# The first block of a recurrence issued in one step, and filling products issued ahead of the normed outputs' steps

## The chip, the cores and the metric

One Trainium2 chip, one core. The time is the device time of one execution in microseconds (us), as a median over runs. A profiled execution gives, beside its own time, the span from its first to its last instruction and every instruction's start and duration. The engines are TensorE (PE; its weight loads are listed as PEld), VectorE (DVE), ScalarE (ACT), GpSimd (POOL) and the queue that issues DMAs (SP).

## The reference

One layer of a residual block on 512 frames of width 1024, in float32: a SwiGLU feed-forward half step, a mixer, and a second SwiGLU half step. Each reads an RMS-normed, scaled and shifted copy of `x` and adds its gated output to `x`. The mixer has two groups of four heads each:

- attention heads (low-rank q and kv, rotary part, block-causal), whose outputs are RMS-normed;
- gated delta-rule heads. A state `S` of 128 x 128 per head goes through the sequence chunk by chunk:

```python
def step(state, inp):
    u_c, wk_c, qd_c, kd_c, qk_c, gl_c = inp
    v_new = u_c - wk_c @ state
    o_c = qd_c @ state + qk_c @ v_new
    state = state * gl_c + kd_c.T @ v_new
    return state, o_c        # the state starts at zero
```

Their outputs are RMS-normed per head and multiplied by SiLU of a gate. `mixed @ w_out`, with both groups side by side, is the mixer's output.

## The kernel before, in words

Activations lie feature-major, 512 frames wide, in 128-row tiles. Each large product is made of three matmuls (`mm3`, L466 to L470): both operands are split into a high and a low part, and high-high, high-low and low-high are accumulated in PSUM. The splits of weights are a ScalarE copy and a VectorE subtraction (L228, L229).

The recurrence uses blocks of 128 frames, so there are four, p = 0 to 3, each with four heads side by side in 512 columns. What happens around it:

- `bases`, `inverse`, `inverse_levels` invert the triangular matrices (L1905 is the last batch of their matmuls). `solve(p)` makes `us[p]` (L1931, copied at L1933) and, from block 1 on, `wk[p]` (L1940, L1942).
- `recur(p)` is a generator of two parts. The first reads the state: `wk` times `S` (L1966), `vn` (L1968), `S` scaled on GpSimd, `q` times `S` (L1974) and its copies on ScalarE (L1976). The second makes the new state (L1981, `S` at L1984 for block 0, L1986 for others) and the block's output (L1989, added at L1993, or copied at L1991 for block 0). Block 0 has no state: its first part issues nothing, but yields.
- `gated_out(p)` norms the output in three steps: squares, sums and the reciprocal root on GpSimd (L2027, L2028, L2003, L214); the scaling `on` (L1475); then transposes (L2012), the gate (`mf`, L2018) and the split into `mh` and `ml` (L2020, L2021), eight pieces on VectorE in all.
- `attended(h)` finishes an attention head in the same way (transposes L2211, `mh` L2216, `ml` L2217).
- `out_attended` are the filling products, called `fill`: w_out's rows for the attention heads, 8 output tiles x 4 heads = 32 steps. A step is one group of three matmuls of 512 columns; every fourth is followed by the update of `x` (L2386). When they are done, `out_half` follows (256 columns, the delta-rule heads, first two blocks), then `out_rest`.
- `early` splits the first weights of the second feed-forward (`fh`, `fl`, L1470, L1471): three generators of three steps, of which the third does nothing; their loads are issued when they are listed.

These are stepped by the loop at the end of `mixer`. `Side.step` advances a list of generators. `gate()` issues the gates' SiLU once attention is done, and afterwards steps the normed outputs (`gated`). What order results:

- TensorE executes in the order in which its instructions are planned. Inside `matmuls_in_order` each matmul is tied behind the one traced before it, except those that `loosely` traces (the remaining solves and attention heads).
- On the other engines, and for loose matmuls, the planner takes at each point the instruction that was traced first among those that its own estimate of times holds ready. Tiles of PSUM (`psb`, 5 banks; `psa`, 3) and SBUF slots are given out in the same pass. So a changed trace order can change the order on VectorE and ScalarE too.

Before the loop one early step is taken; in block 0's first pass the last attention head is finished and `fill` begins.

Of the kernel before, what the change touches and what calls it, by code (L numbers as in the profile page):

```python
# [96 lines left out]
class Block:  # L97
# [1855 lines left out]
    def recur(self, p):  # L1953

        nc = self.nc
        h4 = lambda x: x.rearrange("p (h d) -> p h d", h=4)
        hs = lambda h: slice(h * P, (h + 1) * P)
        S, last = self.S, p == NB - 1
        ts = slice(p * P, (p + 1) * P)
        o = self.slot(s="o")  # L1960
        if S is None:
            vn = self.us[p]
        else:
            pw = self.aux()
            for h in range(4):
                nc.tensor.matmul(pw[:, hs(h)], self.wk[p][:, hs(h)], S[:, hs(h)], start=True, stop=True)  # L1966
            vn = self.slot(s="vn")
            nc.vector.tensor_tensor(out=vn, in0=self.us[p], in1=pw, op=ALU.subtract)  # L1968
            if not last:
                sg = self.slot(s="Sg")  # L1970
                self.mul(h4(sg), h4(S), self.bc(self.gl[:, 4 * p:4 * p + 4], 4), nc.gpsimd)
            pq = self.aux()
            for h in range(4):
                nc.tensor.matmul(pq[:, hs(h)], self.qT[h][:, ts], S[:, hs(h)], start=True, stop=True)  # L1974
            for h in range(4):
                nc.scalar.activation(o[:, hs(h)], pq[:, hs(h)], AF.Copy, scale=self.eG[:, 4 * p + h:4 * p + h + 1])  # L1976
        yield
        if not last:
            pst = self.aux()
            for h in range(4):  # L1980
                nc.tensor.matmul(pst[:, hs(h)], self.kd[p][:, hs(h)], vn[:, hs(h)], start=True, stop=True)  # L1981
            self.S = self.slot(s="S")
            if S is None:
                nc.vector.tensor_copy(self.S, pst)  # L1984
            else:
                nc.vector.tensor_tensor(out=self.S, in0=sg, in1=pst, op=ALU.add)  # L1986
        po = self.aux()
        for h in range(4):
            nc.tensor.matmul(po[:, hs(h)], self.qk[h][:, ts], vn[:, hs(h)], start=True, stop=True)  # L1989
        if S is None:  # L1990
            nc.scalar.copy(o, po)  # L1991
        else:
            nc.vector.tensor_tensor(out=o, in0=o, in1=po, op=ALU.add)  # L1993
        self.o[p] = o
        yield
# [224 lines left out]
    def mixer(self, norms):  # L2220
# [81 lines left out]
        fill = Side()  # L2302
# [9 lines left out]
        def gate_silu(n):  # L2312
            silu(gates[:n], self.att_end)
            del gates[:n]
# [15 lines left out]
        def loosely(side, n):  # L2330
            with self.traced() as block:
                side.step(n)
            self.loose.update(i.name for i in block)

        self.mixed[:4] = [(self.slot(F32R, "mh"), self.slot(F32R, "ml")) for _ in range(4)]
        with self.matmuls_in_order():
            gated, self.gated = Side(), 0

            def gate(n=1):
                if gates and not (att.open or att.todo):  # L2340
                    gate_silu(4)
                elif not gates:
                    gated.step(n)

            for p in range(NB):
                while self.wk[p] is None:
                    loosely(chain, 1)
                for _ in self.recur(p):
                    loosely(chain, 2)
                    loosely(rest, 4)  # L2350
                    gate()
                    early.step()
                    if not rest.open and not rest.todo:
                        fill.step(3)
                gated.add(self.gated_out(p))
                gate()
                if p == 1:
                    def half():
                        while self.gated < 2:
                            yield  # L2360
                        yield from self.out_half()
                    fill.add(half())
            while rest.open or rest.todo:
                loosely(rest, 1)
            gate_silu(4)
            early.flush()
            fill.step(2)
            gated.step()
            fill.step(4)
            gated.flush()  # L2370
            fill.flush()
        with self.in_order({mybir.EngineType.PE: self.last_mm}):
# [99 lines left out]
```

## Time and profile before

| | |
|---|---|
| median of 3 runs | 1030.54 us (1029.92 to 1031.6) |
| profiled execution: time, span | 1030.97 us, 1029.3 us |
| TensorE busy | 1013.7 us (98%) |
| VectorE busy | 774.0 us (75%) |
| ScalarE busy | 504.7 us (49%) |
| GpSimd busy | 30.0 us (3%) |
| recurrence, L1981 of block 0 to L2012 of block 3 | 609.4 to 646.8 us |
| granted TensorE clock | 1.000 |

A row of the order in time reads: start, duration, engine, line, operation, output <- inputs, shape, count, and in brackets how long the engine stood idle before it and what it waited for. Matmuls overlap: the start of one lies before the modelled end of the one ahead, so distances between starts say more than durations. A wait is listed as "engine tile line <- what it waited for: sum, times, longest".

### The profile page before, as it was taken

How to read it: one execution, taken by the hardware profiler on the slowest of the kernel's cores; microseconds unless marked ns; L12 is line 12 of the kernel's file. 1: busy time of each engine (PE TensorE's matmuls, PEld its weight loads, DVE VectorE, ACT ScalarE, POOL GpSimd, SP SyncE). 2: the span in 40 equal slices, each digit the busy share in tenths (PEclk: the TensorE clock that was granted, in tenths of full speed). 3: DMA queues.
4: the chain of work that ended last, by engine and by line, in shares of the span. 5: the costliest groups of instructions: out<-in, count | busy, mean ns of one | idle time of the engine just before them, and what ended most of it. 6: DMA issues, size and time to landing. Idle time of an engine off the chain costs nothing. (4 is left out here: it accounts for less than half of the span.)

```text
span 1029.3 us, 16966 instructions
## 1 busy us (share of the span) xinstructions
PE 1013.7 (98%) x6663; PEld 906.4 (88%) x6663; DVE 774.0 (75%) x1355; ACT 504.7 (49%) x911; POOL 30.0 (3%) x74
## 2 busy tenths in 40 slices
PE   7999999999999999999999989999999999999998
PEld 6788899999887899888888788998999999987887
DVE  4789788887787847868888558677888888788541
ACT  4452455556322226469854464374555555633330
POOL 0000000001100000000000011000000000000000
PEclk9999999999999999999999999999999999999999
DMA  9987234244688735211321121113333334383421
GB/s 321 296 277 255 72 93 122 84 124 117 203 296 297 254 92 160 74 42 42 75 75 42 42 83 41 42 40 95 92 100 106 108 99 120 110 277 93 128 61 31
DMA packets 203773, 130.77 MB, mean 127 GB/s; under 512 B 14241, under 2 KB 188334, under 8 KB 203694
## 3 DMA queue, kind: packets, MB, share of 16 engines
q1 hardware_dynamic: 203694, 129.70, 41.5%
q8 instruction: 52, 0.85, 0.3%
q14 instruction: 27, 0.22, 0.1%
HBM read 127.18 MB, written 2.49 MB: 126 GB/s over the span
## 5 line engine op out<-in xcount | busy, mean ns | idle before, releaser
L228 ACT CAST wh<-wr 128x1024 fp32r<-128x1024 f32 (+1 forms) x93 | 93.8, 1016 | 143.3 <-PE pa L469 108.6
L269 DVE TENSOR_TENSOR wl<-wr,wh 128x1024 fp32r<-128x1024 f32 x96 | 117.4, 1223 | 54.5 <-ACT wh L273 54.5
L229 DVE TENSOR_TENSOR wl<-wr,wh 128x1024 fp32r<-128x1024 f32 (+1 forms) x93 | 108.9, 1177 | 45.5 <-ACT wh L228 45.0
L468 PE MATMUL pa<-hh,wh 128*128 128x512 f32 (+1 forms) x357 | 137.4, 385 | 0.0
L470 PE MATMUL pa<-hh,wl 128*128 128x512 f32 (+1 forms) x357 | 135.2, 379 | 0.0
L469 PE MATMUL pa<-hl,wh 128*128 128x512 f32 (+1 forms) x357 | 134.6, 377 | 0.0
L468 PE MATMUL pa<-ah,wh 128*128 128x512 f32 (+1 forms) x356 | 132.3, 372 | 0.0
L469 PE MATMUL pa<-al,wh 128*128 128x512 f32 (+1 forms) x356 | 131.1, 368 | 0.0
L470 PE MATMUL pa<-ah,wl 128*128 128x512 f32 (+1 forms) x356 | 130.9, 368 | 0.0
L273 ACT CAST wh<-wr 128x1024 fp32r<-128x1024 f32 x96 | 98.2, 1054 | 18.3 <-PE pa L469 10.4
L837 DVE SCALAR_TENSOR_TENSOR aa<-ar,sc,aa 128x512 f32<-128x512 f32 x98 | 73.4, 749 | 8.3 <-DMA ar<-in_w_ada 6.5
L468 PEld LDWEIGHTS pa<-hh,wh 128*128 128x128 f32 x357 | 67.4, 189 | 13.1 <-issue 2.5
L468 PEld LDWEIGHTS pa<-ah,wh 128*128 128x128 f32 x356 | 67.1, 188 | 13.5 <-ACT wh L228 2.5
L470 PEld LDWEIGHTS pa<-hh,wl 128*128 128x128 f32 x357 | 67.2, 188 | 11.9
L470 PEld LDWEIGHTS pa<-ah,wl 128*128 128x128 f32 x356 | 67.1, 188 | 11.2
L469 PEld LDWEIGHTS pa<-hl,wh 128*128 128x128 f32 x357 | 67.4, 189 | 10.7
L469 PEld LDWEIGHTS pa<-al,wh 128*128 128x128 f32 x356 | 67.1, 189 | 10.7
L354 PE MATMUL pa<-hh,wh 128*128 128x256 f32 x240 | 68.0, 283 | 0.0
L354 PE MATMUL pa<-th,wh 128*128 128x256 f32 x240 | 67.9, 283 | 0.0
L354 PE MATMUL pa<-tl,wh 128*128 128x256 f32 x240 | 67.9, 283 | 0.0
L354 PE MATMUL pa<-th,wl 128*128 128x256 f32 x240 | 67.9, 283 | 0.0
L354 PE MATMUL pa<-hh,wl 128*128 128x256 f32 x240 | 67.9, 283 | 0.0
(480 smaller groups left out, 2487.1 us busy)
## 6 DMA issues: line engine op xcount, KB each, us to landing
wr<-in_ffn_w_in SPq DMA_DIRECT2D x79, 512.0 KB
ar<-in_w_ada SPq DMA_DIRECT2D x96, 256.0 KB
wr<-in_ffn_w_out SPq DMA_DIRECT2D x32, 512.0 KB
ar<-in_w_ada SPq DMA_DIRECT2D x22, 512.0 KB
wr<-in_w_in SPq DMA_DIRECT2D x21, 512.0 KB
wr<-in_ffn_w_out SPq DMA_DIRECT2D x16, 384.0 KB
wr<-in_w_out SPq DMA_DIRECT2D x8, 512.0 KB
wr<-in_ffn_w_in SPq DMA_DIRECT2D x8, 384.0 KB
```

The source lines that it names most:

```text
L228: self.nc.scalar.copy(hi, raw)
L229: self.nc.vector.tensor_tensor(out=lo, in0=raw, in1=hi.bitcast(F32), op=ALU.subtract)
L269: sub = lambda out, x, y: nc.vector.tensor_tensor(out=out, in0=x, in1=y, op=ALU.subtract)
L273: nc.scalar.copy(hi[:, :n], raw[:, :n])
L354: nc.tensor.matmul(z, a[:, j, :], b, start=start and j == 0 and i == 0, stop=j == 3 and i == 2, skip_group_check=not start)
L468: mm(out, wh, xh, start=start, stop=False)
L469: mm(out, wh, xl, start=False, stop=False)
L470: mm(out, wl, xh, start=False, stop=stop)
L837: nc.vector.scalar_tensor_tensor(out=acc, in0=a, scalar=sc, in1=acc, op0=ALU.mult, op1=ALU.add)
```

## The change

Three things are changed.

1. `recur` yields after its first part only where there is a state. Block 0 is issued in one step, so the loop's body runs 7 times and not 8.
2. In the body, `gate()` comes behind the filling products and not ahead of them, and `early` isn't stepped in block 0.
3. Behind the loop, six filling steps and not four stand between the last block's scaling and its transposes.

```diff
@@ recur @@
             for h in range(4):
                 nc.scalar.activation(o[:, hs(h)], pq[:, hs(h)], AF.Copy, scale=self.eG[:, 4 * p + h:4 * p + h + 1])
-        yield
+            yield
         if not last:
             pst = self.aux()
@@ mixer @@
                 for _ in self.recur(p):
                     loosely(chain, 2)
                     loosely(rest, 4)
-                    gate()
-                    early.step()
+                    if p:
+                        early.step()
                     if not rest.open and not rest.todo:
                         fill.step(3)
+                    gate()
                 gated.add(self.gated_out(p))
                 gate()
                 if p == 1:
@@ mixer @@
             early.flush()
             fill.step(2)
             gated.step()
-            fill.step(4)
+            fill.step(6)
             gated.flush()
             fill.flush()
```

## The prediction

> **What bounds the kernel now.** I read the page's first two lines, then the stretches around the recurrence, then what TensorE waited for, then the order of instructions on each engine there. The page's lines:
>
> ```profile
> span 1029.3 us, 16966 instructions
> ...
> PE 1013.7 (98%) x6663; PEld 906.4 (88%) x6663; DVE 774.0 (75%) x1355; ACT 504.7 (49%) x911; POOL 30.0 (3%) x74
> ```
>
> TensorE is busy 1013.7 of 1029.3 us, so a change that neither adds nor removes a matmul can win at most its idle time, 15.6 us. The stretches (start:end, length, busy time of PE, PEld, DVE, ACT, POOL, granted clock, DMA) say where that lies:
>
> ```profile
> 593.90:599.40 5.50, 5.10 (x51) 4.25 (x50) 3.26 (x8) 3.29 (x9) 1.01 (x1) 1.00 1.07 326
> 599.40:617.50 18.10, 15.40 (x121) 14.34 (x122) 9.12 (x16) 11.87 (x22) 2.05 (x2) 1.00 0.05 14
> 617.50:637.00 19.50, 19.50 (x128) 17.45 (x126) 16.36 (x38) 10.46 (x28) 4.91 (x4) 1.00 0.10 28
> 637.00:650.00 13.00, 10.71 (x59) 8.99 (x59) 11.46 (x28) 4.39 (x11) 1.01 (x2) 1.00 0.28 82
> 650.00:675.00 25.00, 24.91 (x209) 24.71 (x208) 16.84 (x41) 9.45 (x22) 0.70 (x1) 1.00 0.07 22
> ```
>
> Two stretches have holes, 2.70 and 2.29 us. Between them and after them TensorE has none to speak of (19.50 of 19.50, 24.91 of 25.00), so time won at the holes should reach the end. The clock is full in all of them. TensorE's waits from 585 to 650 us, longest first:
>
> ```profile
> PE pb L2012 <- DVE on L1475: 2.3, 2, 1.5
> PE pb L1966 <- DVE S L1984: 1.5, 1, 1.5
> PE pb L2211 <- DVE on L1475: 1.2, 1, 1.2
> PE pb L2189 <- DVE U L1909: 0.4, 1, 0.4
> ```
>
> L2012 transposes a block's normed output, L1966 is the first product of a recurrence block, L2211 the last attention head's transposes. Where they stand, with the end of the matmul order of before:
>
> ```profile
> 593.95 0.48 PE L468 MATMUL pa<-mh,wh 128*128 128x512 f32 x1
> ...
> 594.73 0.40 PE L468 MATMUL pa<-mh,wh 128*128 128x512 f32 x1
> ...
> 595.51 2.08 PE L1905 MATMUL pb<-U,Y 64*64 64x64 f32 x32
> ...
> 606.79 0.48 PE L468 MATMUL pa<-mh,wh 128*128 128x512 f32 x1
> ...
> 608.91 0.63 PE L2211 MATMUL pb<-ident,on 128*128 128x128 f32 x4 [1.19 <-DVE on L1475]
> 609.38 1.06 PE L1981 MATMUL pb<-uu,kd 128*128 128x128 f32 x8
> 610.27 1.06 PE L1989 MATMUL pb<-uu,qk 128*128 128x128 f32 x8
> ...
> 615.76 1.13 PE L1966 MATMUL pb<-S,w 128*128 128x128 f32 x8 [1.47 <-DVE S L1984]
> ...
> 636.00 1.05 PE L1989 MATMUL pb<-vn,qk 128*128 128x128 f32 x8
> 637.88 0.63 PE L2012 MATMUL pb<-ident,on 128*128 128x128 f32 x4 [0.82 <-DVE on L1475]
> 638.26 0.47 PE L468 MATMUL pa<-mh,wh 128*128 128x512 f32 x1
> ...
> 644.28 0.39 PE L470 MATMUL pa<-mh,wl 128*128 128x512 f32 x1
> 646.14 0.66 PE L2012 MATMUL pb<-ident,on 128*128 128x128 f32 x4 [1.47 <-DVE on L1475]
> ```
>
> The holes are 1.19 + 1.47 + 0.82 + 1.47 = **4.95 us**. The filling products come in groups of three matmuls (L468 to L470); nine of them stand between the last two L2012, from 638.26 to 644.28 + 0.23, so one group is 0.69 us. There are 32 groups before the half-width ones.
>
> **The change part by part.**
>
> *One step for block 0.* Block 0 has no state to read, so the first part of its generator issues nothing; before, the loop still ran its body there, with three groups. They are the ones at 593.95, 594.73 and 606.79. As the loop's matmuls keep their traced order, L1981 of block 0 had to stand behind the third. Now L1981 and L1989 are first in that order and the three groups follow them. Two prices:
>
> The loss. The two groups at 593.95 can no longer be there, since L1981 needs `uu`, which ScalarE copies eight microseconds later. They covered a wait:
>
> ```profile
> 594.56 0.59 ACT L1898 COPY Y<-pb 64x512 f32<-64x512 f32 x1
> ...
> 602.61 0.59 ACT L1933 COPY uu<-pb 128x512 f32<-128x512 f32 x1 [1.06 <-PE pb L1931]
> ...
> 595.51 1.94 PEld L1905 LDWEIGHTS pb<-U,Y 64*64 64x64 f32 x32 [0.36 <-ACT Y L1898]
> ```
>
> L1905 starts when ScalarE's copy is in, groups or not, so the place stays 595.51 and 2 x 0.69 = **1.38 us** of products must be done later. Nothing else stands ready behind them: all later matmuls of the loop are ordered behind L1989. The bounds: at best other loose products (attention's transposes) slip in and nothing is lost, 0; at worst 1.56, the whole 593.95 to 595.51. I take 1.38, the groups' own length.
>
> The gain. L1981 and L1989 (609.38 to 611.16, 1.78 us) move in front of the solves of blocks 2 and 3, and the three groups (2.07 us) stand free to run while L2211 waits for `on`, 1.19 us. For L1966 the profile shows what kept `S`, on VectorE:
>
> ```profile
> 612.95 0.75 DVE L2386 SCALAR_TENSOR_TENSOR xT<-pa,mod,xT 128x512 f32<-128x512 f32 x1 [1.89 <-PE pa L470]
> 614.32 0.69 DVE L1471 TENSOR_TENSOR fl<-fr,fh 128x512 fp32r<-128x512 f32 x1 [0.62 <-ACT fh L1470]
> 614.93 0.68 DVE L1984 COPY S<-pb 128x512 f32<-128x512 f32 x1
> ```
>
> `S` was ready to copy at about 610.4 and was queued behind the first residual update, which waited 1.89 us for the fourth group, and behind a split of an early weight, which waited for ScalarE. Now that fourth group comes behind L1966 and L1974 of block 1, so its update can't stand ahead of `S`, and the split (early.step) isn't taken in block 0 at all. Both holes close: **1.19 + 1.47 = 2.66**. Bounds: 0, if L2211 and `S` are planned as late as before, to 2.66. I take 2.66: behind L1989 there are 2.07 us of groups, eight matmuls of L1940 (0.89, as L1981's eight from 609.38 to 610.27) and L2211's four (0.47) in front of L1966, against 0.68 for the copy. The split left out costs the same 0.69 us later, in the flush behind the loop, under the eight groups there; without them it would stand in the last block's chain. The gates' SiLU moves behind the groups; on ScalarE it waits for the last head anyway. No DMA passes another: the early weights' loads are all issued when their list is made, the groups issue their weights' loads in the same order on SP, and the steps that they pass issue none.
>
> *Groups in front of the normed outputs' steps.* In each pass the three groups now come ahead of gate(), so a block's L2012 stands three groups (2.07 us) later behind L1989. Blocks 0 and 1 waited for nothing. Block 2 waited **0.82** at 637.88 and has 2.07 more: gone.
>
> *Six groups at the last.* Between L1989 of block 3 and its L2012 there stood 9 groups, one L2012 and the 0.82 wait; now 3 + 2 + 6 = 11 groups and one L2012, 11 x 0.69 + 0.38 = 7.97 us. On VectorE the last block's chain ran so:
>
> ```profile
> 638.90 0.68 DVE L1993 TENSOR_TENSOR o<-o,pb 128x512 f32<-128x512 f32 x1
> ...
> 642.32 0.68 DVE L2028 TENSOR_REDUCE gs<-hn 128x4 f32<-128x512 f32 x1
> 642.91 1.22 DVE L229 TENSOR_TENSOR wl<-wr,wh 128x1024 fp32r<-128x1024 f32 x1
> ...
> 645.39 0.69 DVE L1475 TENSOR_TENSOR on<-o,ry 128x512 f32<-128x512 f32 x1 [0.52 <-POOL ry L214]
> ```
>
> From L1989's end (637.05) to `on` (646.08) are 9.03 us, of which 1.85 pass before `o` starts (block 2's late `on` stands ahead) and 2.74 between `o` and `gs`, where ScalarE's square takes 0.63 and block 2's eight pieces and an update the rest:
>
> ```profile
> 639.70 0.63 ACT L2027 ACTIVATE hn<-o 128x512 f32<-128x512 f32 x1 [3.90 <-DVE o L1993]
> ```
>
> With block 2's `on` long done and its transposes 2.07 us behind L1989, `o` can start at once, and `gs` is ready 1.6 us behind L1989 (0.68 + 0.63 and the hops), before those pieces exist. Without these two delays the chain needs 9.03 - 1.85 - (2.74 - 0.75) = about 5.2 us against 7.97: the wait of **1.47** goes. Bounds: +1.47 to a loss of 0.83 (second rival). I take 1.47, since the order of readiness is what the planner goes by.
>
> *The sum:* 4.95 - 1.38 = 3.57 us. The profiled execution took 1030.97 with a span of 1029.3; it becomes 1025.7 in span and 1027.4 in time. It stands 0.43 above the median of the runs, 1030.54, so for the median I say **1027.0 us**. No matmul is added; 3.57 us of waiting go.
>
> **The rivals.**
>
> *The last transposes still wait.* If VectorE's order stays as it was, with block 3's squares behind block 2's pieces, the 8.20 us from L2012 at 637.88 to `on` at 646.08 stay, and the cover behind that L2012 is only 0.38 + 8 x 0.69 = 5.9: a wait of 2.3 in place of 1.47. Then 4.95 - 1.38 - 2.3 = 1.27, or 1029.3 us. For it: pieces come earlier in the program than the squares. Against it: they are ready about a microsecond later.
>
> GpSimd's rsqrt is in this chain:
>
> ```profile
> 634.91 1.22 DVE L229 TENSOR_TENSOR wl<-wr,wh 128x1024 fp32r<-128x1024 f32 x1
> ...
> 635.14 1.86 POOL L214 TENSOR_TENSOR ry<-ve,mhalf 128x4 f32<-128x4 f32 x1 [6.47 <-DVE ve L2003]
> ...
> 644.35 1.01 POOL L214 TENSOR_TENSOR ry<-ve,mhalf 128x4 f32<-128x4 f32 x1 [7.35 <-DVE ve L2003]
> ```
>
> It took 1.86 instead of 1.01 us while a weight split ran on VectorE. If that meets the last one too, 0.85 more comes on: 1030.1 in this rival, nothing in the forecast, which has 2.8 us to spare. [...]
>
> *The first half does nothing.* If L2211 and `S` are planned late for a reason other than the one I read, both holes stay and only the second stretch is won: 0.82 + 1.47 - 1.38 = 0.91, or 1029.6 us. The move to the front of the order speaks against it.
>
> *VectorE becomes the bound: slower.* L2012 now stands right ahead of the next block's L1966, so block p's pieces meet `vn` of block p+2. Their rows:
>
> ```profile
> L2018 DVE SCALAR_TENSOR_TENSOR mf<-pb,cwT,z 128x128 f32<-128x128 f32 x16 | 4.9, 346 | 0.8 <-PE pb L2012 0.8
> L2021 DVE TENSOR_TENSOR ml<-mf,mh 128x128 fp32r<-128x128 f32 x16 | 4.1, 287 | 0.2 <-ACT mh L2020 0.2
> ```
>
> Four of each are 4 x (0.35 + 0.29) = 2.5 us. From L2012's end TensorE has L1966, L1974 and three groups, 1.78 + 2.07 = 3.85 us, before L1981 needs `vn`. Pieces and `vn` (0.69) fit, 3.2; with a weight split (1.22) and an update (0.75) ahead, 5.2, they don't, and 1.35 is waited for in blocks 2 and 3 each, 2.7. With the last transposes late too (a full VectorE makes both) it is 4.95 - 1.38 - 2.3 - 2.7 = -1.43: 1032.0 us. It decides from 0.65 us a block on. For it: VectorE is busy 16.36 of 19.50 in that stretch. Against it: 3.14 are free, and the work is the same, only later by three groups.
>
> **How the numbers follow.** Forecast 0.55 (1026.4 to 1027.9, by what the loss at 593.95 and small delays on VectorE make of it), last transposes 0.20, first half nothing 0.15, slower 0.10. The best end is the loss at 0 and everything closed, 4.95: 1025.6. The upper end takes in the second and third case: 1030.2. About 0.2% (2.1 us) is what a measurement of this kernel tells from no change. The forecast lies below 1028.5, as does a small part of the second case, where some of the wait is left: faster 0.60. The rest of the second, the third, and a third of the slower one (shorter stalls) are within: 0.33. Slower 0.07.
>
> **What would show it.** Right: no group of filling products before L1981 of block 0; a hole of about 1.5 us before L1905; no wait at L2211 and at the first L1966; none at the last two L2012; from 650 on the same steps some 3.6 us earlier. Wrong: a new wait of L1981 for `vn`, of the last L2012 for `on`, or anything in the hole before L1905 that I say can't be there; and a shift that is given back later would be against my reading that TensorE is full behind 650.

## The result, and the profile after

The changed kernel takes **1028.65 us** (median of 16 runs, 1026.54 to 1030.84), the kernel before 1030.59 beside it (16 runs, 1029.92 to 1032.26): a ratio of 0.998, 95% interval 0.9973 to 0.9987. It is faster, by 1.9 us and not by the forecast's 3.5, and by a little less than the 2.1 us that the prediction takes for what a measurement here tells from no change. The profiled execution took 1027.16 us with a span of 1025.4; it is one of the shorter ones.

The first two lines of its page:

```profile
span 1025.4 us, 16972 instructions
...
PE 1014.4 (99%) x6663; PEld 907.5 (88%) x6663; DVE 774.0 (75%) x1355; ACT 504.4 (49%) x911; POOL 29.8 (3%) x74
```

The stretches of the prediction (length, busy time of PE, PEld, DVE, ACT, POOL, granted clock, DMA), and the single microseconds inside the first:

```profile
593.90:599.40 5.50, 4.89 (x44) 4.65 (x45) 3.49 (x9) 2.31 (x5) 1.01 (x1) 0.71 1.07 325
599.40:617.50 18.10, 18.01 (x141) 17.05 (x141) 9.13 (x16) 13.45 (x26) 3.06 (x3) 0.99 0.01 3
617.50:637.00 19.50, 19.50 (x124) 17.01 (x123) 17.80 (x40) 9.63 (x24) 3.44 (x3) 1.00 0.12 35
637.00:650.00 13.00, 13.00 (x84) 11.62 (x83) 11.69 (x30) 5.69 (x14) 1.32 (x1) 1.00 0.28 83
...
595.00:596.00 1.00, 1.00 (x21) 1.00 (x19) 0.82 (x2) 0.49 (x2) 0.00 (x0) 1.00 1.08 317
596.00:597.00 1.00, 1.00 (x12) 0.88 (x10) 0.03 (x1) 0.00 (x0) 0.89 (x1) 0.60 1.10 327
597.00:598.00 1.00, 1.00 (x6) 1.00 (x7) 0.84 (x2) 0.00 (x1) 0.12 (x1) 0.50 1.14 343
598.00:599.00 1.00, 1.00 (x6) 1.00 (x5) 1.00 (x4) 0.63 (x2) 0.00 (x0) 0.50 1.14 344
599.00:600.00 1.00, 1.00 (x8) 0.88 (x7) 1.00 (x3) 0.63 (x3) 0.00 (x0) 0.69 0.36 107
```

The two stretches with holes are full now (18.01 of 18.10, 13.00 of 13.00). But the granted clock, 1.00 in every stretch of before, is 0.71 in the first: it stands at 0.50 from about 596.2 to 599.6. What TensorE waited for from 580 to 655 us is one row:

```profile
PE pb L1905 <- ACT Y L1898: 1.0, 1, 1.0
```

All four of the old waits are gone, and L2189's 0.4 as well. The order of TensorE in the stretches of the change, after:

```profile
593.08 0.44 PE L2183 MATMUL pb<-ident,pr 128*128 128x128 f32 x2
594.51 2.30 PE L1905 MATMUL pb<-U,Y 64*64 64x64 f32 x32 [0.99 <-ACT Y L1898]
596.74 1.22 PE L2189 MATMUL pb<-vn,pT 128*128 128x128 f32 x4
597.75 1.70 PE L2183 MATMUL pb<-ident,pr 128*128 128x128 f32 x7
599.25 2.04 PE L2189 MATMUL pb<-vn,pT 128*128 128x128 f32 x14
601.12 0.60 PE L2211 MATMUL pb<-ident,on 128*128 128x128 f32 x4
...
608.96 0.63 PE L2211 MATMUL pb<-ident,on 128*128 128x128 f32 x4
...
611.51 1.05 PE L1966 MATMUL pb<-S,w 128*128 128x128 f32 x8
...
632.68 1.16 PE L1989 MATMUL pb<-vn,qk 128*128 128x128 f32 x8
...
641.68 0.64 PE L2012 MATMUL pb<-ident,on 128*128 128x128 f32 x4
```

and before, at the same instructions:

```profile
593.75 0.44 PE L2183 MATMUL pb<-ident,pr 128*128 128x128 f32 x2
...
597.52 0.71 PE L2189 MATMUL pb<-vn,pT 128*128 128x128 f32 x4
598.07 0.93 PE L2183 MATMUL pb<-ident,pr 128*128 128x128 f32 x7
599.44 1.80 PE L2189 MATMUL pb<-vn,pT 128*128 128x128 f32 x14 [0.44 <-DVE U L1909]
601.08 0.60 PE L2211 MATMUL pb<-ident,on 128*128 128x128 f32 x4
```

The same instructions last up to 1.8 times as long: four L2189 1.22 for 0.71, seven L2183 1.70 for 0.93. From the start of L1905 to the start of L2211 it is 594.51 to 601.12, 6.61 us, where before took 595.51 to 601.08, 5.57: **1.04 us lost**, with the closed wait of 0.44 in it already.

The whole time of one execution hides much of this. The two transposes ahead of L1905 (the L2183 x2 above), which stand ahead of everything that the change moves, start anywhere between 592.81 and 595.19 us in the 13 profiles of this study. So I also measure from their start to an instruction behind the mixer, VectorE's scaling of the next norm's sums:

```profile
661.95 0.16 DVE L805 TENSOR_SCALAR ve<-pb 128x2 f32<-128x2 f32 x1 [1.74 <-PE pb L754]
```

in before, and in the changed kernel:

```profile
658.16 0.16 DVE L805 TENSOR_SCALAR ve<-pb 128x2 f32<-128x2 f32 x1 [1.74 <-PE pb L754]
```

From there to the end all 13 profiles take 367.2 to 367.4 us. Between the two points before takes 68.20 us and the changed kernel 65.08: **3.12 us won** in this execution, against 3.57 forecast. L805 comes 3.79 us earlier, and the end 3.81: nothing is given back later.

### The profile page after: what moved, and what is told of

Read it like the earlier page. It is cut to its first block, busy times and chain, and to the rows that moved or that the text cites. A ratio compares the mean times of both kernels' runs of the same rounds, so it can differ in the third digit from the quotient of the medians.

```text
span 1025.4 us, 16972 instructions
## 1 busy us (share of the span) xinstructions
PE 1014.4 (99%) x6663; PEld 907.5 (88%) x6663; DVE 774.0 (75%) x1355; ACT 504.4 (49%) x911; POOL 29.8 (3%) x74
## 4 chain that ended last, share of the span: by engine, by line
PE 92%; DVE 4%; ACT 1%; SPq 1%; DMA 1%; issue 0%; POOL 0%; ACTq 0%; DVEq 0%
PE pa L354 17%; PE pa L468 17%; PE pa L469 16%; PE pa L470 16%; PE pb L354 13%; PE pa L1250 1%; PE pb L2189 1%; PE pb L1250 1%; PE pb L468 1%; PE pb L469 1%; PE pb L470 1%; SPq L136 1%; DMA ar<-in_w_ada 1%; PE pb L2169 1%; DVE cv L1687 1%; DVE wl L229 1%
## 5 line engine op out<-in xcount | busy, mean ns | idle before, releaser
L354 PE MATMUL pa<-hl,wh 128*128 128x256 f32 x240 | 67.9, 283 | 0.0
```

The source lines that it names most:

```text
L354: nc.tensor.matmul(z, a[:, j, :], b, start=start and j == 0 and i == 0, stop=j == 3 and i == 2, skip_group_check=not start)
```

## The experiments

Two theories stood after the result. *Clock:* the loss is the half clock behind the new hole before L1905, and the hole sets it off; fill the hole with anything and the forecast's time appears. *Order:* the loss comes from VectorE and the DMAs in the new order, and the low clock only goes along with it. Each run is timed against the kernel before on the same chip.

**The changed kernel once more**, with no edit.

> The changed kernel once more, for its spread. Theory A (the clock): the hole of about 1.4 us that the change opens before L1905 lets the granted TensorE clock fall to one half for some microseconds in most executions, and that costs the median some 1.6 us and makes the times spread; so times from 1026.5 to 1031, median about 1028.6, and the lowest times go with a mean clock of 1.000. Theory B (the order): the missing gain and the spread come from VectorE and the DMAs in the new order, and the lower clock goes along with it; the same median, but no tie between clock and time.

1027.89 us (11 runs), ratio 0.9974 (0.9965 to 0.9983), 0.7 below what either theory expected. Its profile has a clock of 0.996 for the whole, and its windows:

```profile
594.00:595.00 1.00, 0.67 (x9) 0.67 (x10) 0.15 (x2) 0.95 (x3) 0.00 (x0) 0.85 1.10 337
...
595.00:600.00 5.00, 5.00 (x37) 4.84 (x35) 3.83 (x9) 1.05 (x3) 1.01 (x1) 0.50 0.92 271
...
600.00:601.00 1.00, 1.00 (x6) 0.92 (x5) 0.28 (x1) 0.63 (x3) 0.00 (x0) 0.50 0.01 3
601.00:602.00 1.00, 1.00 (x9) 1.00 (x9) 0.46 (x1) 0.77 (x2) 0.00 (x0) 0.74 0.00 0
```

and in its order of matmuls:

```profile
594.33 3.39 PE L1905 MATMUL pb<-U,Y 64*64 64x64 f32 x32 [1.00 <-ACT Y L1898]
...
602.42 0.60 PE L2211 MATMUL pb<-ident,on 128*128 128x128 f32 x4
```

The same hole, but twice the half clock: 0.3 + 5 + 1 + 0.52 = 6.8 us of it (each window's missing clock divided by 0.5), where the first profile has 0.8 + 1 + 1 + 0.62 = 3.4. From L1905 to L2211 it is 8.09 us, 2.52 more than before. From L2211 to L805 the two profiles agree: 57.04 and 57.05 us. So the 1.5 us between them lie where the half clock stands, not in an order behind it.

Over the 27 executions of the changed kernel: five kept a clock of 1.000 and took 1027.40 us in the mean, eight show 0.998 (1027.89), fourteen 0.997 or 0.996 (1028.98). The tie is loose in so few runs: of the three of this run at 1.000, one is the fastest and two stand at its median. All 48 runs of the kernel before that were timed beside the experiments show 0.999 or more.

**The two groups loose again**, so that they may stand in the hole:

```diff
                     if not rest.open and not rest.todo:
-                        fill.step(3)
+                        if not p:
+                            loosely(fill, 2)
+                        fill.step(3 if p else 1)
                     gate()
```

> As the changed kernel, but the first two groups of filling products aren't tied behind L1989 of block 0, so they stand before L1905 again, as in the kernel before. Theory A: clock 1.000 in every execution, all of the 4.95 us won, 1025.6 us, and a spread as small as that of the kernel before (about 2 us). Theory B: the groups' 1.38 us are won and nothing else, about 1027.3 us, with the spread of the changed kernel.

1026.42 us (5 runs), ratio 0.996 (0.9948 to 0.9973), clock 0.999 or more in all five; timed once more, 1026.73. TensorE's only wait left is the L2189 of before. It is the fastest kernel of the study, but the time lies between what the two theories expected, 1025.6 and 1027.3, and the edit moves work too, so it doesn't tell them apart alone.

**One group loose** (`loosely(fill, 1)`, then two).

> As the changed kernel, but one group of the two stands before L1905, so the hole is half as long, about 0.7 us. Theory A: if half the hole keeps the clock up, 1030.6 - 4.95 + 0.69 = 1026.3 us with a clock of 1.000; if it doesn't, 1027.9 with a clock below 1.000. Theory B: 0.69 below the changed kernel, 1027.9, with the same spread.

1026.70 us (6 runs), 0.9965 (0.9953 to 0.9977), clock 0.999 or more. The wait at L1905 is 0.3 and another of 0.8 stands at L2189, 4 us later: about the same idle time as the changed kernel's, in two pieces, and no half clock.

**The hole filled with work that is thrown away.** Everything stays as in the changed kernel; two extra groups, whose sums the next product overwrites, may run in the hole (the products that count are unchanged):

```diff
             p = self.acc()
+            if t == 0:
+                for _ in range(2):
+                    self.dense(p, u[0], self.mixed[4:], k1=1, last=0)
+                yield
             for k in range(4):
@@ mixer @@
                     if not rest.open and not rest.todo:
+                        if not p:
+                            loosely(fill, 1)
                         fill.step(3)
```

> As the changed kernel, with two groups of matmuls whose results are thrown away in the hole before L1905: they compute the first group twice into a tile that the true first group starts anew. No other instruction changes its place. Theory A: the clock stays at 1.000, and the time is that of the forecast, 1030.6 - 3.57 = 1027.0 us, 1.6 below the changed kernel, with a small spread, though more work is done. Theory B: useless work wins nothing, 1028.6 us with the same spread.

1027.14 us (8 runs), 0.997 (0.996 to 0.9981), no execution under 0.999. Six more matmuls, and the time is near the forecast's 1027.0. Between this median and the changed kernel's 1027.89 the intervals overlap; what tells them apart is the clock, 0.999 or more in 8 of 8 against 3 of 11 on the same chip, and the profile. From the transposes to L805 this kernel takes 64.35 us where the changed kernel took 65.08 and 66.57, and from L2211 on it takes the same 57.04 as both. So the order behind the hole is not what costs: the half clock costs 0.73 us in the one profile and 2.22 in the other, against a hole filled with useless work.

**The same with small matmuls**, 22 of 64x64 like those around the hole, meant to last 1.4 us:

```diff
-                for _ in range(2):
-                    self.dense(p, u[0], self.mixed[4:], k1=1, last=0)
+                a = slice(0, 64)
+                for i in range(22):
+                    nc.tensor.matmul(p[a, :64], self.mixed[4][0].bitcast(F32)[a, :64], self.ident[a, a], start=True,
+                                     stop=True)
```

> As the kernel with thrown-away groups in the hole before L1905, but the hole is filled with 22 small matmuls of 64 x 64 x 64, as long as the two groups together (about 1.4 us) and on a quarter of the array, as L1905's are. Theory A1, it is idleness of TensorE that lets the clock fall: clock 1.000 in every execution and 1027.1 us, as with the full-width groups. Theory A2, it is too little work in the array over some microseconds, to which the small matmuls around the hole belong: the clock falls as in the changed kernel, and the time is that of the changed kernel, about 1028 to 1028.6, or worse.

1027.49 us (6 runs), 0.9968 (0.9956 to 0.9981), clock 1.000 in all six. Its order of matmuls and the stretch around it:

```profile
593.49 2.60 PE L2388 MATMUL pa<-ident,mh 64*64 64x64 f32 x41
```

```profile
593.00:598.00 5.00, 5.00 (x83) 4.70 (x81) 2.50 (x6) 2.48 (x6) 1.01 (x1) 1.00 1.04 321
```

(The trace records two for each of these that the program writes, 44 for 22: the 41 of this row and three that stand between L1905's first, at 595.93, 595.99 and 596.05.) They took longer than meant and held L1905 until 595.88, so from the transposes to L805 this kernel, with 65.03, wins no more than the changed one with its 65.08. What it shows is the clock: with 64x64 matmuls in place of the gap it stays at 1.00 in this stretch and at 1.000 over all six executions, where the gap of 0.99 us in the same place was followed by 0.50.

**The one step alone** on the kernel before (`yield` indented, `early` not stepped in block 0).

> The kernel before with the first part of the change alone: block 0 in one step and no early step there; gate() stays ahead of the filling products and four of them stand at the last. By the forecast's terms 2.66 are won at L2211 and the first L1966 and 1.38 lost before L1905, while the waits of 0.82 and 1.47 at the last two L2012 stay: 1030.6 - 1.28 = 1029.3 us. With the clock falling as in the changed kernel (0.8 to 1.5 us) 1030.1 to 1030.8, clock below 1.000. Rival, that the waits move on to the later blocks: 1030.6 or more with a clock of 1.000.

1029.98 us (11 runs), 0.9986 (0.9977 to 0.9995); 10 of the 11 at 0.997 or 0.998. Clock and time go together here: 1028.2 in the one run at 1.000, 1029.03 in the mean of four at 0.998, 1030.35 in that of six at 0.997. Its waits, and then its windows:

```profile
PE pb L2012 <- DVE on L1475: 1.1, 1, 1.1
PE pb L1905 <- ACT Y L1898: 1.0, 1, 1.0
```

```profile
595.00:596.00 1.00, 1.00 (x19) 1.00 (x18) 0.80 (x2) 0.31 (x1) 0.09 (x1) 0.88 0.92 268
...
596.00:599.00 3.00, 3.00 (x18) 2.88 (x17) 2.04 (x6) 0.62 (x2) 0.92 (x1) 0.50 1.12 336
...
599.00:600.00 1.00, 1.00 (x9) 0.81 (x7) 1.00 (x3) 0.71 (x3) 0.00 (x0) 0.92 0.24 70
```

The one step brings hole and half clock (0.24 + 3 + 0.16 = 3.4 us) by itself. It also closes three of the four waits, block 2's L2012 among them; the last one stays, with 1.1.

**The other two parts alone**: the changed kernel with block 0 in two steps again, and its early step.

> The changed kernel without the first part: block 0 in two steps with its early step, but gate() behind the filling products and six of them at the last. No hole before L1905, so the clock stays at 1.000. By the forecast's terms the waits at the last two L2012 go, 0.82 + 1.47 = 2.29, and those at L2211 and the first L1966 stay: 1028.3 us. Rival, that part one made the last waits go too by taking a split off VectorE's list: 1029.1 to 1030 us, with a wait left at the last L2012.

1027.30 us (5 runs), 0.9966 (0.9953 to 0.9978), clock 1.000 in all five: a microsecond better than expected. L2211 waits for 1.2 as before, and a new wait of 0.9 stands at the last L1989 (for `vn`), but the wait at the first L1966 is gone although nothing of block 0 moved. ScalarE's order there:

```profile
610.62 0.63 ACT L201 ACTIVATE z<-z 128x512 f32<-128x512 f32 x1
611.15 0.60 ACT L1470 CAST fh<-fr 128x512 fp32r<-128x512 f32 x1
611.66 1.67 ACT L201 ACTIVATE z<-z 128x512 f32<-128x512 f32 x3
```

and before:

```profile
611.58 2.20 ACT L201 ACTIVATE z<-z 128x512 f32<-128x512 f32 x4
613.68 0.60 ACT L1470 CAST fh<-fr 128x512 fp32r<-128x512 f32 x1
```

Before, the cast that the early split needs stood behind all four gate SiLUs; with gate() behind the groups it stands behind one: 0.53 us after the first SiLU's start and not 2.10. The split comes that much sooner, and `S`, which VectorE copies behind it, is there in time. Moving gate() closes that hole without the one step.

**Four groups at the last**, on the kernel with two loose.

> As the kernel with the first two groups untied (1026.4 us), but four groups and not six between the last block's scaling and its transposes. In the changed kernel's profile the last scaling ends 0.08 us before the last L2012, so with two groups less (1.38 us) about 1.3 us of waiting come back there: 1027.7 us. Rival, the forecast's own estimate that the chain has 2.8 us to spare: no change, 1026.4.

1027.56 us (5 runs), 0.9968 (0.9955 to 0.998), against 1026.42 and 1026.73 with six, each timed at another time; the intervals overlap. The last L2012 waits for its `on` again:

```profile
PE pb L2012 <- DVE on L1475: 1.2, 1, 1.2
```

L1981 waits 0.2 us for `vn` besides. From the transposes to L805 it takes 64.91 us against 63.54 and 63.58 with six: the two more groups are worth 1.3 to 1.4 us.

**gate() in front of the groups again**, on the same kernel, beside that kernel itself.

> Two groups untied, six groups at the last, but the normed outputs' steps in front of each pass's groups again. The forecast gave the groups in front 0.82 us (block 2's L2012) by themselves: by it that wait comes back, 1027.2 us. The reading of the runs so far: where only block 0's step was changed, block 2's `on` was there in time and that wait was gone, so the groups in front are worth nothing of their own behind the one step: at most 0.2 us of wait at block 2's L2012, none at the last one (11 groups still stand ahead of it), 1026.4 to 1026.7.

> The kernel with two groups untied once more, as the measure of the two beside it: 1026.4 us again, clock full. If its earlier lead over the changed kernel was that chip's, it comes out at 1027.5 or more.

1027.89 us (10 runs), 0.9973 (0.9964 to 0.9982), against 1026.73 (5 runs), 0.9963 (0.9949 to 0.9977). Both guesses missed. TensorE's waits at L2012 are back, 0.58 and 0.94 us, but at blocks 0 and 1:

```profile
619.00 0.63 PE L2012 MATMUL pb<-ident,on 128*128 128x128 f32 x4 [0.58 <-DVE on L1475]
...
628.25 0.66 PE L2012 MATMUL pb<-ident,on 128*128 128x128 f32 x4 [0.94 <-DVE on L1475]
```

Block 2 waits for nothing. From the transposes to L805 it takes 65.10 us, 1.52 more than the same kernel with the groups in front (63.58), which is these two waits. I read it so, without a run that tests it: with two groups gone ahead of the loop, TensorE is at block 0's outputs that much sooner, and the three groups in front cover it there.

**The early split in block 0 too** (the condition `if p:` taken away), on the same kernel.

> Two groups untied, and the split of an early weight taken in block 0 too. By the forecast's reading the split keeps S: it waits for ScalarE's half (about 611.8 us where it was taken in block 0), S is copied behind it at 612.4, and L1966, which came at 610.6, waits about 2.5 us: 1028.9. The rival: S is ready 2.5 us before the split and goes ahead of it, no wait at L1966, 1026.4 us.

1026.78 us (5 runs), 0.9962 (0.9948 to 0.9976): the same median as without. VectorE there:

```profile
607.97 0.68 DVE L1984 COPY S<-pb 128x512 f32<-128x512 f32 x1
...
612.03 0.69 DVE L1471 TENSOR_TENSOR fl<-fr,fh 128x512 fp32r<-128x512 f32 x1 [1.70 <-ACT fh L1470]
```

`S` goes four microseconds ahead of the split; it is the earlier state products that free it. But waits of 0.7 (L1981 for `vn`) and 0.4 (last L2012) appear, and from the transposes to L805 this profile takes 64.67 us, 1.09 more than without the split in block 0. The medians of five runs don't show it; whether every execution has these waits is open.

**All profiles on one stretch.** From the start of the two transposes to L2211, and to L805, in us; "won" is against before:

| kernel | to L2211 | to L805 | won |
|---|---|---|---|
| before | 7.33 | 68.20 | |
| changed, 3.4 us of half clock | 8.04 | 65.08 | 3.12 |
| changed, 6.8 us of half clock | 9.52 | 66.57 | 1.63 |
| two groups loose (two profiles) | 7.32 and 7.32 | 63.54 and 63.58 | 4.66 and 4.62 |
| one group loose | 7.29 | 63.63 | 4.57 |
| hole filled with groups | 7.31 | 64.35 | 3.85 |
| hole filled with small matmuls | 8.03 | 65.03 | 3.17 |
| one step alone, 3.4 us of half clock | 8.16 | 66.66 | 1.54 |
| the other two parts alone | 7.31 | 65.08 | 3.12 |
| two loose, four at the last | 7.30 | 64.91 | 3.29 |
| two loose, gate() in front | 7.31 | 65.10 | 3.10 |
| two loose, early split in block 0 | 7.30 | 64.67 | 3.53 |

It is one profile each, but where two have the same order they agree to 0.05 us, apart from the half clock.

## Why the prediction was right or wrong

The sign held, and so did the reading of the four waits; the time is 1.65 us above the forecast's. 1028.65 lies outside the forecast's own 1026.4 to 1027.9 and just above the 1028.5 below which it put 0.60. It lies in the part of the range that is there for two rivals, the last transposes late (1029.3) and the first half for nothing (1029.6), and neither of them happened. That the range held is luck: what filled the distance was in no case of the prediction.

**The four waits: right.** All four closed. From L2211 (601.08 before, 601.12 after) on, the two profiles tell the forecast's sum without the clock: 0.04 us behind at that point, and 3.8 ahead at the end (1030.97 to 1027.16), so 3.85 won against 4.95 - 1.38 = 3.57. The kernel with the hole filled wins the same 3.85 from the transposes to L805.

**The hole before L1905: right in place, too large in size.** Foreseen as 1.5 us, it is 0.99 and the only wait. L1905 did not stay in its place relative to the transposes ahead of it: 593.75 to 595.51 before, 593.08 to 594.51 after, 0.33 us sooner.

**The step that failed: "The clock is full in all of them".** It was true of before and carried silently into the sum after the change. The loss was priced as deferred products only, 0 to 1.56; the hole's second price, the half clock behind it, was in no term and in no bound. From L1905 to L2211 it costs 1.04 us in one profile and 2.52 in another, and it shows in 22 of 27 executions.

What it costs over all runs is an estimate. The profiles with a mean clock of 0.998 have 3.4 us of half clock and the one with 0.996 has 6.8, so I take 0.998 for 1.04 us and 0.997 or 0.996 for 2.52. The first 16 runs have four of the one and ten of the other, 1.8 us in the mean; the 11 later ones have four of each, 1.3 us. The mean times of the two sets of runs are 2.04 and 2.71 us below those of before, so without the half clock 3.9 and 4.0 would have been won. Within the scatter that accounts for the 1.65, and for most of the difference between the two sets. The five runs at a full clock say less themselves, 1027.40 in the mean, 3.3 below before; they scatter by 0.65 and don't settle it.

**"2.8 us to spare" for the last chain: wrong by 2.7.** VectorE and GpSimd in the changed kernel:

```profile
633.82 1.22 DVE L229 TENSOR_TENSOR wl<-wr,wh 128x1024 fp32r<-128x1024 f32 x1
634.96 0.68 DVE L1993 TENSOR_TENSOR o<-o,pb 128x512 f32<-128x512 f32 x1
...
638.05 0.67 DVE L2028 TENSOR_REDUCE gs<-hn 128x4 f32<-128x512 f32 x1
...
640.91 0.69 DVE L1475 TENSOR_TENSOR on<-o,ry 128x512 f32<-128x512 f32 x1 [0.90 <-POOL ry L214]
```

```profile
639.55 1.32 POOL L214 TENSOR_TENSOR ry<-ve,mhalf 128x4 f32<-128x4 f32 x1 [6.37 <-DVE ve L2003]
```

From L1989's end (632.68 + 1.16 = 633.84) to `on` (641.60) are 7.76 us, not 5.2; L2012 follows at 641.68. The cover was right (7.84 against 7.97), so 0.08 is to spare. "`o` can start at once" failed on a weight split of 1.22 that stands in front of it, and "`gs` is ready 1.6 us behind L1989, before those pieces exist" came out as 2.5: ScalarE's square ended at 636.36, when block 2's transposes were done too, and with an update and the first pieces ahead of it `gs` started 4.2 us behind L1989. GpSimd's `ry` took 1.32 beside a split (L1471, 639.32 to 640.01) where the one at 632.17, beside none, took 1.01; with 2.8 to spare that would have been nothing, and here the slack would have been 0.39 without it. The wait did close, but by 0.08 us and not by the reason given: that too was luck.

**The cause of the wait for `S`: half right.** `S` did queue behind the update and the split. But leaving the split out of block 0, which the forecast called part of the cure, isn't needed for it (`S` goes ahead with the split there too), and the wait closes in two independent ways: by the earlier state products, or by gate() moved behind the groups. So 1.47 of the 2.66 put down to the one step was to be had without it.

**The shares: wrong.** Forecast, the one step brings 2.66 - 1.38 = 1.28 us and the rest 2.29. Measured alone, they bring 0.8 (1030.76 to 1029.98) and 3.5 (1030.76 to 1027.30) in the medians, 1.54, with 3.4 us of half clock in it, and 3.12 from the transposes to L805. Together they bring 1.9 and 2.75 in the two sets of runs, and 3.12 or 1.63 on that stretch, by the half clock. The sum isn't reached: they share the waits for `S` and at block 2's L2012, and the one step brings the half clock. As built, the one step wins nothing over the other two parts; with two groups untied all three together win 4.1 to 4.2.

**"VectorE becomes the bound": not here, but real.** Its wait, `vn` behind pieces and splits, is nowhere in the changed kernel. It stands with 0.9 us in the kernel without the one step, with 0.7 in the one with the early split in block 0 and with 0.2 in the one with four groups at the last: in one block each, not in two.

## What to carry to other kernels

A hole that a change opens on TensorE can have two prices, its own length and what the clock does behind it: here 0.99 us, and behind it 1.04 or 2.52 us from L1905 to L2211. The clock of the profile of before, 1.00 in every stretch, said nothing about a hole that wasn't there yet. When products that filled a wait are moved, leave enough of them free to stand there (two groups left so, 1.38 us, kept the clock at 0.999 or more in ten executions), and look at the granted clock in windows of a microsecond: 0.998 over the whole span hid 3.4 us at 0.50. Cost each part alone as well as together: two parts may close the same wait, and then the one that opens a hole may not be worth having. And where executions scatter by more than a change wins, compare the stretch of the profile that the change can reach, between two instructions that it doesn't move.

## What the runs showed of the hardware

Behind a hole of 1.0 us with 64x64 matmuls close by on both sides (L1896, L1905) TensorE's clock fell to half, 1.7, 1.4 and 0.4 us after the hole's end, for 3.4, 3.4 and 6.8 us, in the three profiles that have it; in 32 of the 38 executions of these two kernels the mean clock is 0.998 or less. Holes of 1.19 and 1.47 us in the kernel before, between 128-wide matmuls, left it at 1.00, and so did 0.3 and 0.8 in two pieces 4 us apart, the first in the place of the 1.0.

What sets the drop off stays open. With small matmuls in the place of the 1.0 us, no gap between them, the clock stayed at 1.000 in six executions, and with larger gaps, the 1.19 and 1.47 us among full-width matmuls, it stayed too; so neither the small matmuls alone nor a gap alone brought it in these runs. A gap of the same length moved among full-width matmuls, or a larger one among small ones, wasn't tried. No run shows either why the half clock lasted 3.4 us in two profiles and 6.8 in the third, or why five of the changed kernel's 27 executions have a clock of 1.000.
